# A down projection by seven products over both column halves, in five full K groups and a short last one

## The chip, the cores and the metric

The kernel runs on one core of a Trainium2 chip. The metric is the device time of one execution in microseconds (us). A core has TensorE (PE: matrix products, and PEld, its weight loads), VectorE (DVE), ScalarE (ACT) and GpSimd (POOL), and queues from which transfers are issued; here SyncE's (SP) issues nearly all weight loads and POOL's the transfers that add what they bring to what lies in the destination.

## The reference

Two layers of a decoder trunk over 256 tokens of width 2048, in float32. Layer 0 has a gated DeltaNet beside a latent attention, layer 1 a retention; both end alike, and the change lies in that end alone:

```
u = causal_dwconv(hn @ w_up, conv_w) + conv_b      # w_up: 2048 x 11264, conv width 3
gate, up = jnp.split(u, 2, axis=-1)
h = h + (jax.nn.silu(gate) * up) @ w_down          # w_down: 5632 x 2048
```

A gated per-layer embedding and the next norm follow. With 256 tokens every weight is read about once and used for two blocks of 128 tokens.

## The kernel before

**Precision by splitting.** Each float32 operand is split into a high part (rounded to the matrix engine's format) and a low part (the rest), and a product is the sum of three: high by high, low by high, high by low. For weights `cut` (lines 179 to 195) does it in pieces of 128x1024: ACT casts the piece into a `hi` tile (L188), DVE subtracts it from the raw weights into a `lo` tile (L189). There are four `hi` and four `lo` buffers (`WB`) and four raw buffers of twice that size (`RAWB`).

**The feed-forward layer.** The 5632 inner columns are 44 K tiles of 128. `up` makes them two at a time: each pair takes two `gemm_b` (gate and up half), each of two steps of three yields. One such step is called an *up unit* here: one weight load of 1 MB, two pieces, 16 matmuls of 512 columns (L267) and 16 of 256 (L272). After a `gemm_b` come a copy and an add out of PSUM (L279, L280), a scaling (L282), two scalings on ACT (L1072) and four multiply-adds on DVE (L1074); after both, SiLU, a product (L1084) and the split of the result (L482, L483).

**The down projection** of a group of K tiles runs behind the up projection of the next group. `plain` takes one column block of 512 at a time: for 8 K tiles two units of 24 matmuls (L296, L297, L302), one for each 4 K tiles and both token blocks, and an add into the residual `h` (L1100). `seven` takes two column blocks and 8 K tiles at once as a 2x2 block product (two token blocks, two K halves, two column blocks) by seven block products in place of eight, after Strassen and Winograd. Each is 12 matmuls of 512 columns (L443, L444, L448) and two pieces to split, against one of four left forms made from the activations (`Forms`, L381 to L389) or the activations themselves. The right sides are quadrants of `w_down`, 4 K tiles by 512 columns (1 MB), loaded fresh by SP into a raw buffer (L408), or a running sum T that lies in two tiles: SP writes its first quadrant (L408), and POOL adds further ones by accumulating transfers, two of 512 KB for each quadrant (L412). One product takes B12 + B22, made on DVE (L472).

**The order of the work.** Groups before are K tiles 0-4, 4-12, 12-20, 20-28, 28-36 and 36-44. The four in the middle do column blocks 0 and 1 by `seven` and 2 and 3 by `plain`; the first does all four by `plain`, and the last is a `proj_add` over 8 K tiles that feeds the next norm column by column. `LAG` up units go first; then after each up unit 0.8 units of the group behind it are issued (`SHARE`), in turn one of `plain` and two of `seven`. A scheduler then gives each engine its list in about the order of the code; each engine works its list in order. `then` (before: `following`) starts the next T while the seventh product runs, a whole group ahead of its use.

Of the kernel before, what the change touches and what calls it, by code (L numbers as in the profile page):

```python
# [21 lines left out]
P = 128  # L22
# [10 lines left out]
PSB = 4  # L33
UNIT = 3
LAG = 2
SHARE = 0.8
RATES = [1.7, 1.1, 1.1, 0.95, 2.8]
D = 2048
S = 256
NH = 2  # L40
KB = D // P
CG = 4
EPS = 1e-6
D_FF = 5632
NFT = D_FF // P
# [40 lines left out]
def trunk(ctx: ExitStack, tc: tile.TileContext, a: dict):  # L86
# [12 lines left out]
    V, A, G, T = nc.vector, nc.scalar, nc.gpsimd, nc.tensor  # L99
# [18 lines left out]
    def pb():  # L118
        return psb.tile([P, 512], F32, tag="pb", name=nm("pb"))
# [13 lines left out]
    h = [[None] * CG for _ in range(NH)]  # L133
# [60 lines left out]
    def run(gen):  # L194
        try:
            while True:
                next(gen)
        except StopIteration as e:
            return e.value
# [198 lines left out]
    class Quads:  # L398
# [11 lines left out]
        def plus(self, hh, e):  # L410
            for q in range(2):
                G.dma_start(self.total[q], self.blocks[q, hh, e], accum_op=ALU.add)  # L412

        def begin(self):
            self.put(self.total, 0, 0)
            self.plus(0, 1)

        def fresh(self, hh, e):
            raw = rawp.tile([P, 4, 512], F32, tag="raw", name=nm("raw"))
            dst = [raw[:, 2 * q : 2 * q + 2] for q in range(2)]  # L420
            self.put(dst, hh, e)
            return dst

    def running():
        return [xtile().bitcast(F32).rearrange("p a b c -> p a (b c)") for _ in range(2)]

    def seven(quads, tiles, forms, then):

        c, run_t, fresh, plus = quads.c, quads.total, quads.fresh, quads.plus

        def x(half, i):
            def at(q, k):
                return xl(tiles, 4 * q + 2 * half + k, i)
            return at

        def product(o, left, right, start):
            los = []
            for q in range(2):
                hi, lo = cut(right[q], 2, 512)
                los.append(lo)  # L440
                for k in range(2):
                    l = left(q, k)
                    T.matmul(o, l[0], hi[k], start=start and q + k == 0, stop=False, skip_group_check=True)  # L443
                    last_mm[0] = T.matmul(o, l[1], hi[k], start=False, stop=False, skip_group_check=True)  # L444
                yield
            for q in range(2):
                for k in range(2):
                    last_mm[0] = T.matmul(o, left(q, k)[0], los[q][k], start=False, stop=q + k == 2, skip_group_check=True)  # L448
            yield

        h11, h12, h21, h22 = h[0][c], h[0][c + 1], h[1][c], h[1][c + 1]
        one = pb()
        yield from product(one, forms.left(0), run_t, True)
        V.tensor_sub(h22, h22, one)
        V.tensor_sub(h12, h12, one)
        plus(1, 1)
        acc = pb()
        yield from product(acc, x(0, 0), fresh(0, 0), True)
        V.tensor_add(h11, h11, acc)
        one = pb()  # L460
        yield from product(one, x(1, 0), fresh(1, 0), True)
        V.tensor_add(h11, h11, one)
        yield from product(acc, forms.left(1), run_t, False)
        V.tensor_sub(h12, h12, acc)
        plus(1, 0)
        one = pb()
        b22 = fresh(1, 1)
        yield from product(one, forms.left(3), b22, True)
        V.tensor_sub(h12, h12, one)
        t3 = fresh(0, 1)  # L470
        for q in range(2):
            V.tensor_add(t3[q], t3[q], b22[q])  # L472
        yield from product(acc, forms.left(2), t3, False)
        V.tensor_sub(h22, h22, acc)
        V.tensor_add(h21, h21, acc)
        one = pb()
        yield from product(one, x(1, 1), run_t, True)
        then()
        V.tensor_add(h21, h21, one)

    def put_split(t, k, n, src):
        A.copy(t[:, k : k + n, 0], src)  # L482
# [171 lines left out]
    for g3 in range(3):  # L654
# [14 lines left out]
        ps = run(first_gemm if g3 == 0 else gemm_a(w_in, 0, KB, 4096 + 368 * g3, 368, X))  # L669
# [341 lines left out]
    n = Norm(C_NORM["l0_ffn_norm"])  # L1011
# [44 lines left out]
    def ffn(l, nf, nxt, aside=None):  # L1056
        pin = []
        w_up, w_dn = a[f"l{l}_ffn_w_up"], a[f"l{l}_ffn_w_down"]
        fp = cp.tile([P, N_FFN], F32, name=nm("fp"), tag="fp")
        nc.sync.dma_start(fp, a["par"][:, N_PAR0 + l * N_FFN : N_PAR0 + (l + 1) * N_FFN])  # L1060
        Xf = nf.tiles

        def fc(c):
            return fp[:, c : c + 1]

        def conv(cb, j0):
            ps = yield from gemm_b(w_up, cb, Xf)
            u = joined(ps, nf.bc)
            y = t2((P, 2, S))
            for j in range(2):  # L1070
                ct = j0 + j
                A.activation(y[:, j], u[:, j], AF.Identity, scale=fc(ct + 176), bias=fc(ct + 264))  # L1072
                for lag in range(1, 3):
                    V.scalar_tensor_tensor(y[:, j, lag:], u[:, j, : S - lag], fc(ct + (2 - lag) * 88), y[:, j, lag:], op0=ALU.mult, op1=ALU.add)  # L1074
            return y

        def up(g0, g1, tiles, forms):
            kept = []
            for jp in range(g0, g1, 2):
                tiles.append(xtile())  # L1080
                yg = yield from conv(jp * P, jp)
                yu = yield from conv(D_FF + jp * P, NFT + jp)
                A.activation(yg, yg, AF.Silu)
                V.tensor_mul(yg, yg, yu)  # L1084
                put_split(tiles[-1], 0, 2, yg)
                if forms is not None:
                    kept.append(yg)
                    if len(kept) == 2:
                        forms.add(*kept)
                        kept = []  # L1090

        def down(g0, g1, tiles, forms, quads, then):
            r0, nk = g0 * P, g1 - g0

            def plain(cols):
                for c in cols:
                    ps = [pb() for _ in range(NH)]
                    yield from gemm_a(w_dn, r0, nk, c * 512, 512, tiles, ps)
                    for i in range(NH):
                        V.tensor_add(h[i][c], h[i][c], ps[i])  # L1100

            if forms is None:
                then()
                yield from plain(range(CG))
                return
            fast = seven(quads, tiles, forms, then)
            slow = plain(range(2, CG))
            going = True
            while going:
                going = False  # L1110
                for part in (slow, fast, fast):
                    for _ in range(UNIT):
                        if next(part, part) is not part:
                            going = True
                            yield

        groups = [(max(g - 4, 0), g + 4) for g in range(0, NFT, 8)]
        prev = None
        total = []

        def following(g0):
            if g0 + 8 < NFT:
                if not total:
                    total.extend(running())
                quads.append(Quads(w_dn, g0 * P, 0, total))
                quads[-1].begin()

        quads = []
        for g0, g1 in groups:
            forms = Forms() if 0 < g0 and g1 < NFT else None  # L1130
            cur = (g0, g1, [], forms)
            going = up(g0, g1, cur[2], forms)
            if prev is not None:
                behind_it = down(*prev, quads[-1] if quads else None, partial(following, g0))
                for _ in range(LAG * UNIT):
                    next(going)
                owed = 0.0
                for n, _ in enumerate(going, 1):
                    if n % UNIT:
                        continue  # L1140
                    owed += SHARE
                    if owed >= 1.0:
                        owed -= 1.0
                        for _ in range(UNIT):
                            next(behind_it, None)
                run(behind_it)
            else:
                run(going)
            if g0 == 4 and aside is not None:
                aside()  # L1150
            if g1 + 8 == NFT:
                pin.append(ple_input(l))
            prev = cur
        later(lambda: pin.append(ple_tiles(pin.pop())))
        run(proj_add(w_dn, [(prev[0] * P, prev[2], prev[1] - prev[0])], range(CG), nxt.feed))
        later(nxt.finish)
        return pin[0]
# [337 lines left out]
```

## Time and profile before

| | us |
|---|---|
| median of 3 runs (lowest, highest) | 2880.49 (2878.83, 2880.64) |
| the profiled execution's own time | 2880.58 |
| its span, first to last instruction | 2878.8 |

| engine | busy in the span |
|---|---|
| PE | 2860.8 us, 99% |
| PE weight loads | 2464.2 us, 86% |
| DVE | 2060.9 us, 72% |
| ACT | 1537.8 us, 53% |
| POOL | 121.8 us, 4% |

Busy time is the union of an engine's instructions; neighbours overlap (the next begins before the last one's results are out), so the step from start to start is shorter than an instruction's own time. An average over the program says little on one stage: the feed-forward layers are read by windows.

### The profile page before, as it was taken

What the parts mean: (1) busy time and instruction counts of PE and PEld (TensorE: products, weight loads), DVE (VectorE), ACT (ScalarE), POOL (GpSimd) and SP (SyncE); (2) the same over time, 40 slices, a digit from 0 to 9 for tenths busy, and PEclk for the clock granted to TensorE, in tenths of its full rate; (3) what the DMA queues carried; (4) which work ended last, traced back from release to release, by engine and by line L of the source; (5) the groups of instructions that cost most, each with busy time, mean ns of one, the idle gap of its engine ahead of it and who ended that gap; (6) DMA issues with size and microseconds to landing.
All of it is one profiled execution on the core that took longest, in us unless ns stands there. A gap on an engine that the chain in (4) does not pass through costs nothing.

```text
span 2878.8 us, 38652 instructions
## 1 busy us (share of the span) xinstructions
PE 2860.8 (99%) x15076; PEld 2464.2 (86%) x15076; DVE 2060.9 (72%) x2898; ACT 1537.8 (53%) x2185; POOL 121.8 (4%) x116
## 2 busy tenths in 40 slices
PE   9999999999999999999999999999999999999998
PEld 8899988888888888888888888888888888888887
DVE  7888867778878887656556565655668878788765
ACT  7666655555555555554444444344545555555554
POOL 0111100000000000000000000000000000000000
PEclk9999999999999999999999999999999999999999
DMA  7444445757878787555555555555575777877654
GB/s 236 135 132 131 138 161 194 221 189 203 249 206 235 233 232 225 171 183 192 179 185 186 191 181 182 186 179 189 186 222 185 220 232 223 238 220 223 212 185 145
DMA packets 410040, 562.49 MB, mean 195 GB/s; under 512 B 10752, under 2 KB 266880, under 8 KB 409856
## 3 DMA queue, kind: packets, MB, share of 16 engines
q1 hardware_dynamic: 393376, 530.05, 56.2%
q0 software_dynamic: 13056, 25.17, 5.3%
q10 hardware_dynamic: 3424, 4.79, 0.5%
q8 instruction: 118, 1.93, 0.3%
q14 instruction: 66, 0.54, 0.1%
HBM read 557.87 MB, written 2.10 MB: 195 GB/s over the span
## 4 chain that ended last, share of the span: by engine, by line
PE 98%; DVE 1%; ACT 0%; DMA 0%; issue 0%; POOL 0%; ACTq 0%; POOLq 0%; DVEq 0%
PE pa L267 30%; PE pa L272 16%; PE pa L297 10%; PE pa L296 10%; PE pa L302 10%; PE pb L297 3%; PE pb L296 3%; PE pb L302 3%; PE pb L444 2%; PE pb L443 2%; PE pb L448 2%; PE pb L739 2%; PE pb L316 1%; PE pa L936 1%; PE pb L745 0%; PE pb L1234 0%
## 5 line engine op out<-in xcount | busy, mean ns | idle before, releaser
L189 DVE TENSOR_TENSOR lo<-raw,hi 128x1024 fp32r<-128x1024 f32 (+3 forms) x1140 | 1197.9, 1075 | 555.8 <-ACT hi L188 498.8
L188 ACT CAST hi<-raw 128x1024 fp32r<-128x1024 f32 (+3 forms) x1140 | 1010.0, 931 | 955.5 <-PE pa L297 327.6
L267 PE MATMUL pa<-xg,hi 128*128 128x512 f32 x3840 | 925.9, 392 | 0.0
L267 PEld LDWEIGHTS pa<-xg,hi 128*128 128x128 f32 x3840 | 709.7, 188 | 140.6 <-DVE xg L321 0.3
L296 PE MATMUL pa<-hi,xg 128*128 128x512 f32 (+1 forms) x1348 | 522.8, 388 | 2.0 <-ACT hi L188 1.9
L297 PE MATMUL pa<-hi,xg 128*128 128x512 f32 (+1 forms) x1348 | 521.4, 387 | 0.3 <-DVE xg L321 0.2
L272 PEld LDWEIGHTS pa<-xg,lo 128*128 128x128 f32 x3840 | 490.3, 191 | 16.3
L272 PE MATMUL pa<-xg,lo 128*128 128x256 f32 x3840 | 502.0, 283 | 0.0
L302 PE MATMUL pa<-lo,xg 128*128 128x512 f32 (+1 forms) x1348 | 331.7, 386 | 0.0
L296 PEld LDWEIGHTS pa<-hi,xg 128*128 128x128 f32 x1348 | 253.9, 188 | 50.5 <-ACT hi L188 2.2
L297 PEld LDWEIGHTS pa<-hi,xg 128*128 128x128 f32 x1348 | 253.7, 188 | 49.4 <-DVE xg L321 0.8
L302 PEld LDWEIGHTS pa<-lo,xg 128*128 128x128 f32 x1348 | 250.1, 188 | 47.9
L1074 DVE SCALAR_TENSOR_TENSOR t<-t,fp,t 128x255 f32<-128x255 f32 (+1 forms) x352 | 154.0, 479 | 49.8 <-ACT t L1072 48.5
L297 PE MATMUL pb<-hi,xg 128*128 128x512 f32 x348 | 135.9, 391 | 0.0
L296 PE MATMUL pb<-hi,xg 128*128 128x512 f32 x348 | 135.8, 390 | 0.0
L279 ACT COPY t<-pa 128x512 f32<-128x512 f32 x128 | 75.1, 587 | 76.8 <-PE pa L272 67.6
L412 POOL DMA_DIRECT2D xg<-in_l_ffn_w_down_dram x48 | 57.9, 1206 | 1174.5 <-DVE t L1074 419.9
L1072 ACT ACTIVATE t<-t,fp 128x256 f32<-128x256 f32 x176 | 96.1, 593 | 13.4 <-DVE t L282 13.4
L157 POOL TENSOR_TENSOR small<-small,mhalf 128x1 f32<-128x1 f32 (+2 forms) x38 | 28.8, 757 | 1401.1 <-DVE small L1264 622.6
L280 DVE TENSOR_TENSOR t<-t,pa 128x512 f32<-128x512 f32 x128 | 87.1, 680 | 1.1 <-ACT t L279 1.1
L302 PE MATMUL pb<-lo,xg 128*128 128x512 f32 x348 | 86.5, 389 | 0.0
L321 DVE SCALAR_TENSOR_TENSOR xg<-pb,par,xg 128x256 fp32r<-128x256 f32 x136 | 60.0, 479 | 35.8 <-ACT xg L320 35.0
(280 smaller groups left out, 2233.8 us busy)
## 6 DMA issues: line engine op xcount, KB each, us to landing
raw<-in_l_ffn_w_up_dram SPq DMA_DIRECT2D x176, 1024.0 KB, 5.2
raw<-in_l_w_in_dram SPq DMA_DIRECT2D x128, 1024.0 KB, 5.1
raw<-in_l_ffn_w_down_dram SPq DMA_DIRECT2D x56, 1024.0 KB, 5.2
raw<-in_l_w_out_dram SPq DMA_DIRECT2D x44, 1024.0 KB, 5.1
raw<-in_l_ffn_w_down_dram SPq DMA_DIRECT2D x64, 512.0 KB, 4.9
raw<-in_l_ple_gate_dram SPq DMA_DIRECT2D x32, 1024.0 KB, 5.1
xg<-in_l_ffn_w_down_dram POOLq DMA_DIRECT2D x48, 512.0 KB, 6.8
xg<-in_l_ffn_w_down_dram SPq DMA_DIRECT2D x16, 512.0 KB, 4.6
```

Source lines behind the costliest of these rows:

```text
L188: last_cast[0] = A.copy(vo(hi)[:, c], vi(rk)[:, c])
L189: last_diff[0] = V.tensor_sub(vo(lo)[:, c], vi(rk)[:, c], vo(hi)[:, c].bitcast(F32))
L267: last_mm[0] = T.matmul(ps[:, j], wh, x2, start=first, stop=False)
L272: last_mm[0] = T.matmul(ps[:, j, :S], lo[k][:, j * P : (j + 1) * P], xr(tiles, c * 8 + k)[1], start=False, stop=c == 1 and k == 7)
L279: A.copy(u, ps[:, :, S:])
L280: V.tensor_add(u, u, ps[:, :, :S])
L296: T.matmul(o[i], xh, hi[k], start=begin and k0 + k == 0, stop=False)
L297: last_mm[0] = T.matmul(o[i], xw, hi[k], start=False, stop=False)
L302: last_mm[0] = T.matmul(o[i], xl(tiles, k0 + k, i)[0], lo[k], start=False, stop=end and k0 + k == nkb - 1)
L321: V.scalar_tensor_tensor(t[:, kk, 1], pk, g, t[:, kk, 0].bitcast(F32), op0=ALU.mult, op1=ALU.subtract)
L1072: A.activation(y[:, j], u[:, j], AF.Identity, scale=fc(ct + 176), bias=fc(ct + 264))
L1074: V.scalar_tensor_tensor(y[:, j, lag:], u[:, j, : S - lag], fc(ct + (2 - lag) * 88), y[:, j, lag:], op0=ALU.mult, op1=ALU.add)
```

## The change

Groups become K tiles 0-8, 8-16, 16-24, 24-32, 32-40 (five of 8) and 40-44 (one of 4). Groups 0 to 3 do both pairs of column blocks by `seven`, one after the other; group 4 does blocks 0 and 1 by `seven` and 2 and 3 by `plain`; the last is a `proj_add` over 4 K tiles. So there are nine column halves by seven products in a layer where there were four. The share follows from the group's work: 14 units over the 14 up units left after `LAG`, or 11 over 6 for group 4. One T serves all halves in turn, so a second half's T is begun while the first half's seventh product runs, and used by the next product. T's first product is now the quadrant B11 itself, and each further quadrant (B12, B22, B21) is added after the product that used the sum so far:

| product | right side before | right side now |
|---|---|---|
| 1 | T = B11 + B12 | T = B11 |
| 2 | B11 fresh | B21 fresh |
| 3 | B21 fresh | T, + B12 |
| 4 | T, + B22 | B22 fresh |
| 5 | B22 fresh | T, + B22 |
| 6 | B12 + B22 on DVE | B12 + B22 on DVE |
| 7 | T, + B21 | T, + B21 |

A half reads seven quadrants in place of eight, adds three of them by POOL as before, and makes seven additions out of PSUM in place of nine.

```diff
         def begin(self):
             self.put(self.total, 0, 0)
-            self.plus(0, 1)
...
-    def seven(quads, tiles, forms, then):
-
+    def seven(ready, tiles, forms, then):
+
+        quads = ready.popleft()
...
-        one = pb()
-        yield from product(one, forms.left(0), run_t, True)
-        V.tensor_sub(h22, h22, one)
-        V.tensor_sub(h12, h12, one)
-        plus(1, 1)
         acc = pb()
-        yield from product(acc, x(0, 0), fresh(0, 0), True)
+        yield from product(acc, x(0, 0), run_t, True)
         V.tensor_add(h11, h11, acc)
+        plus(0, 1)
         one = pb()
         yield from product(one, x(1, 0), fresh(1, 0), True)
         V.tensor_add(h11, h11, one)
+        two = pb()
+        yield from product(two, forms.left(0), run_t, True)
+        V.tensor_sub(h22, h22, two)
+        plus(1, 1)
+        b22 = fresh(1, 1)
+        yield from product(two, forms.left(3), b22, False)
+        V.tensor_sub(h12, h12, two)
+        t3 = fresh(0, 1)
+        for q in range(2):
+            V.tensor_add(t3[q], t3[q], b22[q])
         yield from product(acc, forms.left(1), run_t, False)
         V.tensor_sub(h12, h12, acc)
         plus(1, 0)
...
         yield from product(acc, forms.left(2), t3, False)
         V.tensor_sub(h22, h22, acc)
+        yield from product(acc, x(1, 1), run_t, False)
+        then()
         V.tensor_add(h21, h21, acc)
...
-        groups = [(max(g - 4, 0), g + 4) for g in range(0, NFT, 8)]
+        groups = [(g, min(g + 8, NFT)) for g in range(0, NFT, 8)]
+        by_seven = {g0: [0, 2] if n < len(groups) - 2 else [0] for n, (g0, g1) in enumerate(groups[:-1])}
+        jobs = deque((g0, c) for g0, cols in by_seven.items() for c in cols)
...
+        def following():
+            if not total:
+                total.extend(running())
+            if jobs:
+                g0, c = jobs.popleft()
+                ready.append(Quads(w_dn, g0 * P, c, total))
+                ready[-1].begin()
+
+        def down(g0, g1, tiles, forms):
+            fast = chain(*[seven(ready, tiles, forms, following) for _ in by_seven[g0]])
+            rest = [c for c in range(CG) if c - c % 2 not in by_seven[g0]]
+            slow = plain(g0, g1, tiles, rest)
+            parts = [slow, fast, fast] if rest else [fast]
...
-            forms = Forms() if 0 < g0 and g1 < NFT else None
+            forms = Forms() if g1 < NFT else None
...
+                share = sum(7 if c in by_seven[prev[0]] else 2 for c in range(0, CG, 2)) + 2 * (len(by_seven[prev[0]]) == 1)
+                share /= 2 * (g1 - g0) - LAG
```

ACT's list, layer 0, before: from a seventh product's casts of T (the two tiles `xg_5608` and `xg_5609`) on; `raw` pieces are loaded weights, L279 and L1072 belong to the convolution, L388 to the left forms.

```order
L188 CAST hi_7513<-xg_5608 128x1024
L188 CAST hi_7521<-xg_5609 128x1024
L188 CAST hi_7573<-raw_7571 128x1024
L188 CAST hi_7577<-raw_7571 128x1024
L279 COPY t_1341_7533<-pa_7391 128x512
L188 CAST hi_7615<-raw_7613 128x1024
L188 CAST hi_7619<-raw_7613 128x1024
L1072 ACTIVATE t_1342_7537<-t_1341_7533,fp_4995 128x256 x2
L188 CAST hi_7669<-raw_7667 128x1024
L188 CAST hi_7673<-raw_7667 128x1024
L482 CAST xg_7268<-t_1319_7384 128x2x256
L388 CAST t_1345_7554<-t_1343_7548 128x512
```

The next cast of T stands 23 rows after the first of these, behind six further pairs of weight casts.

ACT's list, layer 0, now, at the same step: the casts of T (`xg_5118`, `xg_5119`) for a first half's seventh product, and for the second half's first product.

```order
L187 CAST hi_6450<-xg_5118 128x1024
L187 CAST hi_6458<-xg_5119 128x1024
L1068 ACTIVATE t_1166_6380<-t_1165_6376,fp_4995 128x256 x2
L187 CAST hi_6472<-raw_6470 128x1024
L187 CAST hi_6476<-raw_6470 128x1024
L478 CAST xg_6097<-t_1144_6235 128x2x256
L187 CAST hi_6516<-xg_5118 128x1024
L387 CAST t_1169_6397<-t_1167_6391 128x512
L187 CAST hi_6524<-xg_5119 128x1024
L387 CAST t_1170_6398<-t_1168_6392 128x512
```

Between the two uses of T now stand the casts of one up unit; the second use must wait for the new quadrant, and the left forms' casts (L387) stand behind it.

SP's list, layer 0, before, around the start of a new T:

```order
L169 DMA raw_7571<-in_l_ffn_w_up_dram 128x8x256
L169 DMA raw_7613<-in_l_ffn_w_up_dram 128x8x256
L169 DMA raw_7667<-in_l_ffn_w_up_dram 128x8x256
L169 DMA raw_7709<-in_l_ffn_w_up_dram 128x8x256
L408 DMA xg_5608<-in_l_ffn_w_down_dram 128x2x512
L408 DMA xg_5609<-in_l_ffn_w_down_dram 128x2x512
L169 DMA raw_7753<-in_l_ffn_w_down_dram 128x4x512
L169 DMA raw_7804<-in_l_ffn_w_up_dram 128x8x256
```

SP's list, layer 0, now, around the start of the second half's T:

```order
L168 DMA raw_6470<-in_l_ffn_w_up_dram 128x8x256
L168 DMA raw_6548<-in_l_ffn_w_up_dram 128x8x256
L407 DMA raw_6594<-in_l_ffn_w_down_dram 128x2x512 x2
L168 DMA raw_6617<-in_l_ffn_w_up_dram 128x8x256
L407 DMA xg_5118<-in_l_ffn_w_down_dram 128x2x512
L407 DMA xg_5119<-in_l_ffn_w_down_dram 128x2x512
L168 DMA raw_6698<-in_l_ffn_w_up_dram 128x8x256
L407 DMA raw_6743<-in_l_ffn_w_down_dram 128x2x512 x2
```

The transfer into T moved from between up loads and a plain block to a place with an up load and a fresh quadrant right behind it; ahead of it stand the loads of the next up units and of the second half's first fresh quadrant (`raw_6594`).

## Rows read from the trace of the kernel before

**Rows 1.** The page's head: span; busy time, share and instructions of each engine.
```profile
span 2878.8 us, 38652 instructions
...
PE 2860.8 (99%) x15076; PEld 2464.2 (86%) x15076; DVE 2060.9 (72%) x2898; ACT 1537.8 (53%) x2185; POOL 121.8 (4%) x116
```

**Rows 2.** The page's part 4: the chain that ended last, by engine.
```profile
PE 98%; DVE 1%; ACT 0%; DMA 0%; issue 0%; POOL 0%; ACTq 0%; POOLq 0%; DVEq 0%
```

**Rows 3.** The list of waits, TensorE, whole program: total, times, longest; first of nine.
```profile
PE pa L296 <- ACT hi L188: 1.9, 1, 1.9
```

**Rows 4.** Timeline of TensorE: start, time, then line, operation, tiles, count.
```profile
679.49 0.40 PE L443 MATMUL pb<-hi,xg 128*128 128x512 f32 x1
...
681.33 1.07 PE L448 MATMUL pb<-lo,xg 128*128 128x512 f32 x4
682.24 3.79 PE L267 MATMUL pa<-xg,hi 128*128 128x512 f32 x16
...
687.77 0.40 PE L296 MATMUL pb<-hi,xg 128*128 128x512 f32 x1
...
693.24 3.79 PE L267 MATMUL pa<-xg,hi 128*128 128x512 f32 x16
```

**Rows 5.** Windows, one period of layer 0: busy per engine, PEclk, DMA, GB/s.
```profile
689.87:819.74 129.87, 129.87 (x694) 112.50 (x693) 105.29 (x138) 73.68 (x90) 7.18 (x6) 1.00 0.76 227
```

**Rows 6.** Groups of VectorE in that period: busy, mean ns, idle before.
```profile
L189 DVE TENSOR_TENSOR lo<-raw,hi 128x1024 fp32r<-128x1024 f32 x48 | 57.9, 1219 | 15.2 <-ACT hi L188 15.2
...
L472 DVE TENSOR_TENSOR raw<-raw,raw 128x1024 f32<-128x1024 f32 x2 | 2.4, 1218 | 0.0
```

**Rows 7.** Timeline of VectorE in that period.
```profile
692.53 0.69 DVE L1100 TENSOR_TENSOR t<-t,pb 128x512 f32<-128x512 f32 x1 [2.62 <-PE pb L302]
693.14 2.35 DVE L189 TENSOR_TENSOR lo<-raw,hi 128x1024 fp32r<-128x1024 f32 x2
695.41 0.68 DVE L1100 TENSOR_TENSOR t<-t,pb 128x512 f32<-128x512 f32 x1
```

**Rows 8.** The list of waits of VectorE in that period.
```profile
DVE lo L189 <- ACT hi L188: 15.2, 9, 2.5
DVE t L1100 <- PE pb L302: 5.0, 2, 2.6
DVE t L1074 <- ACT t L1072: 3.4, 3, 1.2
```

**Rows 9.** DMA in that period: queues, then issues with us to landing.
```profile
q1 hardware_dynamic: 21498, 26.24, 60.9%
q0 software_dynamic: 1632, 3.15, 14.9%
...
xg<-in_l_ffn_w_down_dram POOLq DMA_DIRECT2D x6, 512.0 KB, 6.6
xg<-in_l_ffn_w_down_dram SPq DMA_DIRECT2D x2, 512.0 KB, 4.3
```

**Rows 10.** Timeline of VectorE around a seventh product.
```profile
759.43 2.36 DVE L189 TENSOR_TENSOR lo<-xg,hi 128x1024 fp32r<-128x1024 f32 x2
761.70 0.68 DVE L1100 TENSOR_TENSOR t<-t,pb 128x512 f32<-128x512 f32 x1
```

**Rows 11.** Timeline of TensorE at the same place.
```profile
759.53 3.79 PE L267 MATMUL pa<-xg,hi 128*128 128x512 f32 x16
```

**Rows 12.** Line 408 (loads of quadrants), whole program: landing.
```profile
DMA to landing us min/median/max: 3.7/4.9/7.5
```

**Rows 13.** Line 412 (accumulating transfers), whole program: issue ns min/median/max; landing.
```profile
L412 POOL DMA_DIRECT2D xg<-in_l_ffn_w_down_dram x48: 1194/1203/1366, 542.9 to 2666.9; - x48
...
DMA to landing us min/median/max: 5.7/6.8/10.2
```

**Rows 14.** Windows: output projection that feeds the first feed-forward norm.
```profile
462.00:500.00 38.00, 38.00 (x206) 31.68 (x205) 32.61 (x58) 25.96 (x49) 0.70 (x1) 1.00 0.67 219
```

**Rows 15.** Windows: eight microseconds with a high DMA share, layer 0.
```profile
1104.00:1112.00 8.00, 8.00 (x45) 6.92 (x44) 7.72 (x11) 5.00 (x7) 0.00 (x0) 1.00 1.03 263
```

More of the change, by code (lines that the diff above doesn't have):

```diff
@@ L35 @@
 LAG = 2
-SHARE = 0.8
 RATES = [1.7, 1.1, 1.1, 0.95, 2.8]
@@ L465, in seven @@
         plus(1, 0)
[L466 to L472, printed above, removed]
         yield from product(acc, forms.left(2), t3, False)
         V.tensor_sub(h22, h22, acc)
+        yield from product(acc, x(1, 1), run_t, False)
+        then()
         V.tensor_add(h21, h21, acc)
[L476 to L479, printed above, removed]
     def put_split(t, k, n, src):
@@ L1090, in up, with plain @@
                         kept = []
[L1092 to L1107, printed above, removed]
+        def plain(g0, g1, tiles, cols):
+            for c in cols:
+                ps = [pb() for _ in range(NH)]
+                yield from gemm_a(w_dn, g0 * P, g1 - g0, c * 512, 512, tiles, ps)
+                for i in range(NH):
+                    V.tensor_add(h[i][c], h[i][c], ps[i])
+        groups = [(g, min(g + 8, NFT)) for g in range(0, NFT, 8)]
+        by_seven = {g0: [0, 2] if n < len(groups) - 2 else [0] for n, (g0, g1) in enumerate(groups[:-1])}
+        jobs = deque((g0, c) for g0, cols in by_seven.items() for c in cols)
+        ready = deque()
+        total = []
+        def following():
[10 more added lines that the diff above has]
+            parts = [slow, fast, fast] if rest else [fast]
             going = True
@@ L1110, in down @@
                 going = False
-                for part in (slow, fast, fast):
+                for part in parts:
                     for _ in range(UNIT):
@@ L1115, in down @@
                             yield
-        groups = [(max(g - 4, 0), g + 4) for g in range(0, NFT, 8)]
         prev = None
[L1119 to L1129, printed above, removed]
-            forms = Forms() if 0 < g0 and g1 < NFT else None
+        for n, (g0, g1) in enumerate(groups):
+            forms = Forms() if g1 < NFT else None
             cur = (g0, g1, [], forms)
             going = up(g0, g1, cur[2], forms)
[L1133 to L1136, printed above, removed]
+            for _ in range(LAG * UNIT):
+                next(going)
+            if prev is None:
+                following()
+                run(going)
+            else:
+                behind_it = down(*prev)
+                share = sum(7 if c in by_seven[prev[0]] else 2 for c in range(0, CG, 2)) + 2 * (len(by_seven[prev[0]]) == 1)
+                share /= 2 * (g1 - g0) - LAG
                 owed = 0.0
-                for n, _ in enumerate(going, 1):
-                    if n % UNIT:
+                for m, _ in enumerate(going, 1):
+                    if m % UNIT:
                         continue
-                    owed += SHARE
-                    if owed >= 1.0:
+                    owed += share
+                    while owed >= 1.0:
                         owed -= 1.0
@@ L1146, in ffn @@
                 run(behind_it)
-            else:
-                run(going)
-            if g0 == 4 and aside is not None:
+            if n == 1 and aside is not None:
                 aside()
-            if g1 + 8 == NFT:
+            if n == len(groups) - 2:
                 pin.append(ple_input(l))
```

## The prediction

> **What bounds the kernel now.** I read first the page's busy times and its chain. TensorE is busy 2860.8 of 2878.8 us [rows 1] and holds 98% of the chain that ended last [rows 2]. A busy share may hide waits, so the list of waits comes next: TensorE waited nine times for something the profile names, 1.9 us at most [rows 3], and none of these lies in a feed-forward layer. Its granted clock there is 1.00, the 2.4 GHz level [rows 5]. So in the layer that changes the time is a count of matmuls, and two questions are left: how many go, and whether VectorE or the transfers, which get more to do, start to hold TensorE up.
>
> The timeline of TensorE gives the step of each kind of work from start to start [rows 4]: a product of `seven` 679.49 to 682.24, 2.75 us; an up unit 682.24 to 687.77, 5.53; a plain unit 687.77 to 693.24, 5.47. One group's work repeats every 129.87 us (I call it a period); in it VectorE is busy 105.29 us, ScalarE 73.68, and the DMA engines 0.76 of the time at 227 GB/s [rows 5].
>
> **What goes and comes on TensorE.** A column half by `plain` is two blocks of two units: 4 x 5.47 = 21.88. By `seven` it is 7 x 2.75 = 19.25. The difference is 2.63 us. It agrees with the count, 96 matmuls against 84, since 12 matmuls at 5.47/24 = 0.228 are 2.74. A layer has nine halves by seven in place of four, so two layers have ten more: 10 x 2.63 = 26.3 us less. Nothing else on TensorE changes in number. As TensorE sets the end, the whole of it counts unless a new wait gives some back.
>
> **VectorE.** A period in which two halves run by seven has 129.87 - 21.88 + 19.25 = 127.2 us of TensorE. On VectorE the added half has 14 subtractions of 1024 for 8, two sums of 1024 more (L472), and the period has 14 additions out of PSUM for 13. Large ones last 1.22 us [rows 6] but step 2.27/2 = 1.135 back to back, an addition 0.61 [rows 7]. So 8 x 1.135 + 0.6 = 9.7, and VectorE has 115.0 of 127.2 us, 90% where it had 81%. ScalarE gets six casts, about 6 us, 63%. There are four such periods in a layer, eight in all. Of VectorE's idle time now, 15.2 us are waits for a cast [rows 8], and these end with ScalarE, which itself waits until TensorE frees a `hi` buffer: that is slack. 5.0 are for a plain unit's end, which goes, and 3.4 for the convolution on ScalarE, which stays. 115.0 + 3.4 fits. Bursts (two convolution ends and the left forms) are covered by four `lo` buffers, two units of work ahead. Bound below: 0. Bound above: all waits but the 5.0 stay, 15.2 + 3.4 = 18.6 on 115.0, that is 133.6 - 127.2 = 6.4 a period, 51 in all. The waits that the rows show are buffer waits, so I take the lower end, with 1 us for stray ones.
>
> **The turn of T.** This is the one dependency that got much shorter. In layer time let 0 be the end of the sixth product. An up unit ends at 5.5, the seventh product at 8.3, another up unit at 13.8; then the second half's first product needs T again. Its second tile is needed at 13.8 + 0.9 = 14.7 (high part, after half of the 1.84 us of high matmuls [rows 4]) and at 16.1 (low part, 13.8 + 2.3). When is it there? Before, VectorE had split T for a seventh product 2.2 us after the same point (759.53 [rows 11] to 761.70 [rows 10]). Now the sixth product's addition and four multiply-adds of the convolution come ahead or between, 0.6 + 1.6, so 4.5. SP can issue the load of the second tile then. It lands 4.3 us later in this period's median [rows 9], 7.5 in the worst case of line 408 [rows 12]; a cast of about 1.0 and a subtraction of 1.14 follow, and some 1.8 of left forms stand between. So the low part is ready at 4.5 + 4.3 + 3.9 = 12.7, or 15.9 at worst, against 16.1. I take 0. The bounds are 0 and, with the longest landing of any transfer of quadrants, 10.2 [rows 13], 18.6 - 16.1 = 2.5 for each of eight turns, 20 in all. Nothing below 0: no load gets earlier by it. Behind the waiting transfer on SP's queue stand an up load and a fresh quadrant; their uses come two units or more later, and three loads stand ahead of it.
>
> **The other waits added.** An accumulating transfer must now land within two products and two up units where a load alone must at the turn within one of each: 8.3 us more time, against two issues of 1.2 and a landing of 6.6 for 4.3 [rows 9, 13], 4.7 us more work. It has 3.6 us more to spare than the turn, so nothing. POOL has 12 issues a period, 14 us of 127. A sum in PSUM is now carried on after it has been read (products 4 to 7); an up unit of 5.53 stands between read and next write, against an addition of 0.61, so nothing in the eight periods. In group 4 the pace is 11 units to 6 up units, two products can stand side by side, and product 6 must wait until VectorE has read product 5: 0 to 2 us in each layer, I take 1, so 2. The last projection has half as many matmuls between two feeds of the norm; the nearest row is the output projection with only two K blocks to a column and the same feed, where TensorE was busy 38.00 of 38.00 us [rows 14]. It costs 0. Starting with 8 K tiles of up projection alone in place of 4 only moves work.
>
> **DMA.** The plain queue moves 26.24 MB in 60.9% of 130 us, 3.0 us a MB of all engines' time; the accumulating one 3.15 MB in 14.9%, 6.15 a MB [rows 9]. A period now moves 25.2 and 6.3 MB: 76 + 39 = 115 of 127.2 us, a share of 0.90, at 247 GB/s. For 8 us the trace shows 1.03 at 263 GB/s without a wait of TensorE [rows 15]. Loads land in 5 us and are asked for some units ahead, so I take 0. The Trainium skill (Perfetto Trace Analysis, Identifying the Most-Contended Engine) says to judge DMA by bytes moved against what the memory gives, since occupancy of 16 engines misleads. By that rule 247 of the 358 GB/s it gives as a core's share would be 69%, and the transfers would not be a suspect at all. By that rule rival 3 below would have no chance; the rows, where an added byte costs the engines twice a loaded one, leave it one.
>
> **Sum.** The profiled execution took 2880.58 us, its span 2878.8 plus 1.8 around it, 0.1 from the median of 2880.49. 2880.6 - 26.3 + 1 + 0 + 2 + 0 = 2857.3; I say 2857.
>
> **Rivals.** (1) The turn of T comes late: landings stretch to 8 to 10 us as the transfers go from 0.76 to 0.90. From 7.7 us on each us costs 8; at 10.2 it is 20 and the time 2877. Against it: 4.3 in the median at 0.76, and 7.5 as the longest of 80 [rows 9, 12]. (2) The other side: VectorE becomes the bound. Its order holds convolution, split and evacuation in one line, and if its waits stay as long as before (18.6 a period) the work cannot be packed. From 12.2 us of waits a period TensorE stalls; the gain is gone at 15.1; at 18.6 the time is 2854.3 + 51 + 2 = 2907, slower by 0.9%. For it: VectorE has only 12 us of room. Against it: most of those waits are for buffers. (3) The DMA engines hold the pace: if they sustain less than 0.90 a period takes 115/share; at 0.85 it is 135.3, 8.1 more, 65 in all, 2921. For it: three of a half's seven quadrants go the dear way. Against it: 1.03 in [rows 15]. That matmuls saved would turn out to be hidden, or not saved, I give nothing: the count of 120 is fixed by the code and TensorE has no idle time to hide in.
>
> **How the numbers follow.** The forecast, 2854 to 2863, has 64%. Rival 1 has 14%, mostly between 2863 and 2874; rival 2 has 13%, of which 4 in the part that still leaves a gain, 4 about level and 5 slower; rival 3 has 6%, 5 of them slower; 3% are for something unnamed. A measurement of this kernel can tell about 0.2%, 5.8 us, from no change. Faster than 2874.7: 64 + 12 + 4, 80%. Within: 2 + 4 + 1 + 1, 8%. Slower: 12%. The range 2851 to 2876 holds the forecast, nearly all of rival 1 and the mild part of rival 2, some 81%; its lower end is the sum with no loss, 2854.3, less 3 for steps read to 0.02 us.
>
> **What would show it.** In the changed profile: a period of 127 us in place of 129.87 and PE matmuls fewer by 120; VectorE near 115 us in it; DMA share near 0.90. At the turn the first product's casts of T should not end a wait of TensorE; if they do, with T's load behind them, rival 1 holds. Waits of TensorE for `lo` (L188 of the changed kernel) all over the period mean rival 2, waits of ScalarE for raw loads rival 3. The prediction is wrong if TensorE's waits in the two layers sum to more than 20 us.

## The result, and the profile after

The changed kernel took 2853.72 us in the median of four runs (2853.67 to 2855.67). The kernel before, on the same chip, took 2880.46 (2878.83 to 2880.64). The ratio is 0.991, with a 95% interval of 0.9893 to 0.9927. So it is faster by 26.7 us. Executions of one kernel differ by up to 2 us among themselves (before 2878.8 or 2880.4 to 2880.6, changed 2853.7 or 2855.7), so that like with like the gain is some 25 us, and one of the ten executions of the first experiment below, at 10215 us, is left out of its ratio.

The head of the page after, with its chain by engine, answers to [rows 1, 2]. Busy time, share of the span and instructions follow each engine's name.

```profile
span 2852.0 us, 38914 instructions
...
PE 2832.8 (99%) x14956; PEld 2440.3 (86%) x14956; DVE 2163.5 (76%) x3016; ACT 1606.0 (56%) x2253; POOL 194.6 (7%) x176
...
PE 98%; DVE 1%; ACT 1%; DMA 0%; issue 0%; POOL 0%; ACTq 0%; POOLq 0%; DVEq 0%
```

TensorE lost 120 matmuls (15076 to 14956) and 28.0 us of busy time. VectorE gained 102.6 us, ScalarE 68.2 and GpSimd 72.8, and all of that is beside TensorE: the chain is 98% TensorE still.

The list of waits of TensorE over the whole program answers to [rows 3]: total, times, longest.

```profile
PE pa L295 <- ACT hi L187: 1.9, 1, 1.9
...
PE pa L296 <- DVE xg L479: 1.4, 2, 0.7
```

Nine rows again. The second one shown is the only one in the feed-forward layers: 0.7 us in each, at the last projection, where a matmul waits for an activation just evacuated.

Three successive periods of layer 0 answer to [rows 5]; the marks are the starts of VectorE's first addition out of PSUM (L453) in a group's first half, one in a period. Columns: length, then busy time and instructions of TensorE, its weight loads, VectorE, ScalarE and GpSimd, granted clock, DMA share, GB/s.

```profile
590.42:718.06 127.64, 127.64 (x684) 110.64 (x683) 115.53 (x149) 80.17 (x97) 14.45 (x12) 1.00 0.90 248
718.06:845.20 127.14, 127.14 (x682) 110.24 (x681) 114.31 (x147) 80.07 (x96) 14.51 (x12) 1.00 0.89 248
845.20:972.30 127.10, 127.10 (x681) 110.23 (x680) 114.43 (x147) 80.34 (x96) 14.48 (x12) 1.00 0.89 248
```

The period went from 129.87 to 127.1 us with TensorE busy through all of it, at the granted clock of 1.00.

DMA in the second of these periods (each queue's packets, MB and share of the 16 engines' time, then issues with KB each and the median us to landing) answers to [rows 9].

```profile
q1 hardware_dynamic: 20993, 25.17, 59.5%
q0 software_dynamic: 3264, 6.29, 29.2%
...
raw<-in_l_ffn_w_up_dram SPq DMA_DIRECT2D x16, 1024.0 KB, 6.3
...
xg<-in_l_ffn_w_down_dram POOLq DMA_DIRECT2D x12, 512.0 KB, 7.2
xg<-in_l_ffn_w_down_dram SPq DMA_DIRECT2D x4, 512.0 KB, 6.6
```

Twice the accumulating bytes cost nearly twice the time: 6.29 MB in 29.2% of 127.1 us is 5.9 us a MB, against 3.0 for plain loads. The median of 6.6 us for the loads that begin T mixes two kinds. Line 407 at the turn between two halves of one group, in this period, shows

```profile
DMA to landing us min/median/max: 4.6/4.9/5.1
```

At the eight turns these loads land in 3.8 to 5.1 us, as they did before (4.3 [rows 9]). Those that begin T for a next group land in 7.8 to 9.9 us, and T's low part is there some 5 us before it is used.

One wait on VectorE has grown. At product 6 its sum B12 + B22 (L467) waits for the second of the two quadrants (VectorE's list of waits in the second period: total, times, longest):

```profile
DVE raw L467 <- DMA raw<-in_l_ffn_w_down_dram: 3.5, 1, 3.5
```

Before, it waited 4.6 us in the whole program, and not at all in the period of [rows 6]. Now it waits 24.8 us in all, 1.8 to 3.5 in each of the six periods of equal work (three in each layer), and no matmul waits behind it.

### The profile page after: what moved, and what is told of

It is laid out like the page before. It is cut to its first block, busy times and chain, and to the rows that moved or that the text cites. A ratio compares the mean times of both kernels' runs of the same rounds, so it can differ in the third digit from the quotient of the medians.

```text
span 2852.0 us, 38914 instructions
## 1 busy us (share of the span) xinstructions
PE 2832.8 (99%) x14956; PEld 2440.3 (86%) x14956; DVE 2163.5 (76%) x3016; ACT 1606.0 (56%) x2253; POOL 194.6 (7%) x176
## 4 chain that ended last, share of the span: by engine, by line
PE 98%; DVE 1%; ACT 1%; DMA 0%; issue 0%; POOL 0%; ACTq 0%; POOLq 0%; DVEq 0%
PE pa L266 30%; PE pa L271 16%; PE pa L301 10%; PE pa L296 10%; PE pa L295 10%; PE pb L443 4%; PE pb L442 4%; PE pb L447 4%; PE pb L735 2%; PE pb L315 1%; PE pb L296 1%; PE pb L295 1%; PE pb L301 1%; PE pa L932 1%; PE pb L741 0%; PE pb L1232 0%
## 5 line engine op out<-in xcount | busy, mean ns | idle before, releaser
L188 DVE TENSOR_TENSOR lo<-raw,hi 128x1024 fp32r<-128x1024 f32 (+3 forms) x1104 | 1153.7, 1069 | 473.7 <-ACT hi L187 399.9
L187 ACT CAST hi<-raw 128x1024 fp32r<-128x1024 f32 (+3 forms) x1104 | 971.2, 927 | 816.6 <-PE pa L296 328.9
L295 PE MATMUL pa<-hi,xg 128*128 128x512 f32 (+1 forms) x1284 | 497.6, 388 | 2.0 <-ACT hi L187 1.9
L296 PE MATMUL pa<-hi,xg 128*128 128x512 f32 (+1 forms) x1284 | 495.6, 386 | 1.7 <-DVE xg L479 1.4
L301 PE MATMUL pa<-lo,xg 128*128 128x512 f32 (+1 forms) x1284 | 315.8, 386 | 0.0
L295 PEld LDWEIGHTS pa<-hi,xg 128*128 128x128 f32 x1284 | 241.2, 188 | 48.6 <-ACT hi L187 2.2
L296 PEld LDWEIGHTS pa<-hi,xg 128*128 128x128 f32 x1284 | 241.2, 188 | 48.2 <-DVE xg L479 2.3
L301 PEld LDWEIGHTS pa<-lo,xg 128*128 128x128 f32 x1284 | 238.1, 188 | 45.3
L411 POOL DMA_DIRECT2D xg<-in_l_ffn_w_down_dram x108 | 130.7, 1225 | 1187.1 <-DVE lo L188 795.8
L188 DVE TENSOR_TENSOR lo<-xg,hi 128x1024 fp32r<-128x1024 f32 x144 | 173.8, 1218 | 14.5 <-ACT hi L187 14.1
L187 ACT CAST hi<-xg 128x1024 fp32r<-128x1024 f32 x144 | 146.7, 1050 | 58.1 <-PE pb L443 29.9
L443 PE MATMUL pb<-hi,t 128*128 128x512 f32 x288 | 113.1, 393 | 0.0
L442 PE MATMUL pb<-hi,t 128*128 128x512 f32 x288 | 113.0, 392 | 0.0
L279 DVE TENSOR_TENSOR t<-t,pa 128x512 f32<-128x512 f32 x128 | 86.9, 679 | 1.1 <-ACT t L278 1.1
```

What stands on the lines that cost most here:

```text
L187: last_cast[0] = A.copy(vo(hi)[:, c], vi(rk)[:, c])
L188: last_diff[0] = V.tensor_sub(vo(lo)[:, c], vi(rk)[:, c], vo(hi)[:, c].bitcast(F32))
L295: T.matmul(o[i], xh, hi[k], start=begin and k0 + k == 0, stop=False)
L296: last_mm[0] = T.matmul(o[i], xw, hi[k], start=False, stop=False)
L301: last_mm[0] = T.matmul(o[i], xl(tiles, k0 + k, i)[0], lo[k], start=False, stop=end and k0 + k == nkb - 1)
```

## The experiments

**The theories.** A, that of the prediction: time is TensorE's count of matmuls; each half moved from `plain` to `seven` is worth some 2.7 us as long as T is there at the turn, and the new order of the products is what makes it be there. Against it: the order alone, or something beside the count, brought the gain; VectorE was the edge already (rival 2 of the prediction); the DMA engines were (rival 3). The experiments ran in two further sets, in which the kernel before took 2879.17 and 2879.44 us in place of 2880.46, so a difference from the changed kernel's 2853.72 us is uncertain by about 1 us.

**One half in place of two.** The new code, with only the first column half of groups 0 to 3 by seven products: five such halves a layer in place of nine.

```
-        by_seven = {g0: [0, 2] if n < len(groups) - 2 else [0] ...}
+        by_seven = {g0: [0] ...}
```

> The changed kernel, but every full K group does only column blocks 0 and 1 by seven products and blocks 2 and 3 plainly: five halves by seven in a layer in place of nine, eight fewer in both layers. Theory A (the time is the count of matmuls, a half by seven saves 21.88 - 19.25 = 2.63 us): 8 x 2.63 = 21.0 us more than the changed kernel's 2853.7, so 2874.7. Rival (the gain came from the new groups, the short last one above all, and not from the halves): near 2855 to 2860.

Measured: 2875.78 us, ratio to before 0.9989 (0.9979 to 0.9998). The profiled spans are 2873.9 and 2852.0, so eight halves are worth 21.9 us, 2.74 each: the count of 12 matmuls at 0.228 us, to the last digit. Theory A holds, and the second half is where nearly all of the gain lies. TensorE waits nowhere in the layers but for the same 0.7 us at their ends. The new groups bring no gain of their own: this kernel has 24 matmuls fewer than the one before, 5.5 us, and its span is 3.4 us shorter than that of the new order alone (2877.3, third experiment), so the groups cost about 2 us, of which 1.4 are those waits.

**The old order of the products, both halves by seven.** T is again B11 + B12 before the first product that uses it.

```
     def begin(self):
+        self.plus(0, 1)
     ...  (and the old body of seven)
```

> The changed kernel with the old order inside a half: T is B11 + B12 before the first product uses it. At the turn T's load is then followed by an accumulating transfer: 2.4 us of issues and about 7 us to land behind the 4.6 us of the load. In the changed profile the last subtraction of T at a turn ended 14.3 us after the sixth product's end and is needed at 16.1. Theory A (the turn is the tight place, and starting T with one quadrant is what makes it fit): 14.3 + 8.4 to 9.4 is late by 6.6 to 7.6 us at each of eight turns, 53 to 61 us more than 2853.7: 2907 to 2915, and TensorE waits at the turns. Rival (the turn has room enough, or other work fills it): 2853 to 2857.

Measured: 2939.12 us, ratio 1.0206 (1.0186 to 1.0227), 85 us above the changed kernel. The wait at the turn has the predicted size. This is TensorE's longest row of waits (total, times, longest):

```profile
PE pb L443 <- ACT hi L187: 58.1, 16, 5.1
```

58.1 us in eight turns is 7.3 each, two waits to a turn. ScalarE's rows at one turn name what it waits for, the transfers into T:

```profile
646.87 1.04 ACT L187 CAST hi<-xg 128x1024 fp32r<-128x1024 f32 x1 [5.96 <-DMA xg<-in_l_ffn_w_down_dram]
...
652.92 1.04 ACT L187 CAST hi<-xg 128x1024 fp32r<-128x1024 f32 x1 [5.01 <-DMA xg<-in_l_ffn_w_down_dram]
```

But 58 is not 85. The rest is in TensorE's timeline and in the windows of the same stretch (columns as above):

```profile
647.97 0.80 PE L443 MATMUL pb<-hi,t 128*128 128x512 f32 x1 [3.04 <-ACT hi L187]
648.56 0.63 PE L444 MATMUL pb<-hi,t 128*128 128x512 f32 x1
648.99 0.63 PE L443 MATMUL pb<-hi,t 128*128 128x512 f32 x1
...
654.01 0.79 PE L443 MATMUL pb<-hi,t 128*128 128x512 f32 x1 [3.97 <-ACT hi L187]
```

```profile
644.00:650.00 6.00, 2.96 (x12) 1.88 (x10) 1.23 (x1) 1.04 (x1) 0.52 (x1) 0.83 0.98 244
650.00:654.00 4.00, 0.04 (x1) 0.00 (x0) 0.01 (x1) 1.08 (x2) 0.67 (x1) 0.50 0.97 170
654.00:658.00 4.00, 3.98 (x9) 3.14 (x10) 4.00 (x5) 4.00 (x5) 1.20 (x1) 0.50 0.30 44
```

After the waits TensorE's granted clock is 0.50, the 1.2 GHz level, and in 654 to 658 it gets through nine matmuls, 0.43 us apart in place of 0.23. A whole period shows both parts:

```profile
598.30:735.85 137.55, 130.54 (x682) 112.15 (x681) 116.94 (x152) 80.00 (x96) 14.43 (x12) 0.96 0.87 245
```

Against 127.14 it has 7.0 us without work and 3.4 more of work for the same 682 matmuls; 10.4 in each of eight periods would be 83. So the new order (with the eighth quadrant and the two additions that the old one brings back) is worth 85 us here, and the rival that it costs or brings nothing falls. My expectation had the wait and missed the clock.

**The new order alone.** The kernel before (one half by seven in its four middle groups) with T begun as the first quadrant.

```
     def begin(self):
-        self.plus(0, 1)
     ...  (and the new body of seven)
```

> The kernel before with nothing changed but the order inside a half and T's first quadrant (groups and halves as before). Theory A: no matmul less, T begun a whole group ahead: 2880.5, within 1 us. Rival (two additions fewer on VectorE in each half, or shorter PSUM use, give part of the gain): 2 to 5 us less.

Measured: 2880.01 us, ratio 1.0003 (0.9993 to 1.0012). The order brings nothing where only one half of a group runs by seven products, and by the code the plain half beside it gives T's transfers four units more; nothing waited for them before [rows 3]. With the run before it: neither part gains alone, and the two together gain 26.7 us.

**VectorE more loaded.** Behind each product a reduction of 128x512 on VectorE, whose result nobody uses; once in the first kernel, twice in the second.

```
+    spare = cp.tile([P, 1], F32, name="spare", tag="spare")
 ...
+            for _ in range(1):   # 2 in the second
+                V.tensor_reduce(spare, los[1][1].bitcast(F32), axis=AX.X, op=ALU.add)
```

> The changed kernel with one more VectorE instruction behind each product: a sum over 512 columns of its last low part into one spare column that nobody reads, about 0.6 us, 14 in a period, 8.4 us: VectorE has 114.4 + 8.4 = 122.8 of 127.1 us. Theory A (VectorE has room; its waits are for buffers): no more than 3 us above 2853.7. Rival 2 (VectorE cannot be packed that tight): its other waits, 3.4 to 7 us a period, no longer fit, 0 to 3 us a period over and more in bursts: 10 to 40 us more.

> As the run with one more VectorE instruction behind each product, but with two of them: 16.8 us in a period, 114.4 + 16.8 = 131.2 us of VectorE work for 127.1 of TensorE. Theory A (VectorE binds only when its own work is more than TensorE's): 4 us more in each of eight periods and little elsewhere, about 32 us, 2886. Rival 2 (unavoidable waits of 3.4 to 7 us come on top): 60 to 90 us more, 2914 to 2944. If VectorE were far from the bound: no change.

Measured: 2861.76 us (ratio 0.9937, 0.9918 to 0.9957), 8 above the changed kernel; and 2914.13 us (1.0119, 1.0099 to 1.0139), 60 above it. Two periods of the first kernel, then one of the second:

```profile
590.27:718.80 128.53, 128.03 (x684) 110.57 (x683) 123.69 (x163) 79.80 (x97) 14.53 (x12) 1.00 0.88 246
...
2275.87:2402.81 126.94, 126.94 (x681) 110.07 (x680) 122.54 (x161) 79.89 (x96) 14.57 (x12) 1.00 0.89 249
```

```profile
590.65:725.82 135.17, 130.67 (x682) 111.56 (x681) 130.42 (x175) 80.55 (x96) 14.52 (x12) 0.99 0.84 233
```

The period less VectorE's busy time is VectorE's idle time. In the second kernel it is 4.75 us in the period shown and 3.0 to 5.3 in the six periods of equal work, and TensorE idles 4 to 5 us in each of them: there VectorE sets the pace, and 3 to 5 us of its waits are not packed. (The period is 8.0 us longer than the changed kernel's; 4.5 are TensorE's idle time, and its 682 matmuls take 3.5 us longer, at a granted clock of 0.99.) In the first kernel VectorE's idle time is 4.4 to 5.9 us, but TensorE waits only 0 to 1.1 us a period, and not at all in the second row: this kernel stands at the edge. In the second kernel's period VectorE's waits are for ScalarE above all (total, times, longest):

```profile
DVE t L1074 <- ACT t L1072: 2.3, 1, 2.3
DVE lo L188 <- ACT hi L187: 2.0, 1, 2.0
```

In the first kernel's first period they are for a TensorE unit and a load, 2.1 and 1.9, so their cause is not one thing. In the second kernel TensorE waits for VectorE's splits all over the layers (whole program):

```profile
PE pa L271 <- DVE lo L188: 19.9, 21, 2.0
```

Here A's expectation was wrong: it gave VectorE all the idle time of a period, and in the second kernel the rival's reading came out, by which waits are added to the work. In the first the measured 8 lies between the two. The changed kernel is still on A's side: with 3.0 to 5.3 us of such waits, its 114.4 us of work come to 117.4 to 119.7 of 127.1, so some 7 to 10 us of room; the first kernel added 8.1 and stood at the edge.

**More transfers.** Two plain loads of 176 KB behind each product, from ScalarE's queue into spare tiles; a one-column copy of ScalarE orders their reuse. To make room for the tiles, four of eight small buffers (`T1B`) that serve other parts of the layers are given up, which was not measured by itself; so only the feed-forward periods are compared.

```
-T1B = 8
+T1B = 4
 ...
+            for j in range(2):
+                spare.append(spare.popleft())
+                A.copy(spare[-1][:, :1], hi[1][:, :1].bitcast(F32))
+                nc.scalar.dma_start(spare[-1], quads.blocks[0, 0, 0][:, j, :352])
```

> The changed kernel with two more plain loads of 180 KB behind each product, from ScalarE's queue into spare tiles that nobody reads (a one-column copy on ScalarE ahead of each ties it to its place; four small buffers of the mixers are given up for the room, so only the feed-forward periods are compared). 14 x 0.36 = 5.05 MB in a period, at 3.0 us a MB 15.1 us: a DMA share of 0.89 + 0.12 = 1.01 and 288 GB/s. Rival 3 (the engines' busy share is what binds): the transfers hold the pace, periods of 129 to 133 us, 15 to 50 us more in all, waits of TensorE at the turns first. The other reading (bytes against what memory gives, 288 of 358 GB/s): periods stay at 127.1 within 0.5 us.

Measured: 2881.28 us (2874.76 to 2886.28), ratio 1.0001 (0.9991 to 1.0011), 27 above the changed kernel. The profiled execution is the longest of the eight, 2886.28. Its six periods of equal work, then the queues in the first of them:

```profile
592.59:725.30 132.71, 131.14 (x690) 113.13 (x689) 115.80 (x148) 83.59 (x127) 14.45 (x12) 0.99 0.97 277
725.30:856.64 131.34, 128.02 (x681) 110.04 (x680) 114.57 (x147) 82.97 (x124) 14.50 (x12) 1.00 0.98 279
856.64:984.22 127.58, 127.49 (x681) 110.24 (x681) 114.58 (x147) 83.23 (x124) 14.48 (x12) 1.00 1.00 287
2157.37:2294.71 137.34, 131.94 (x689) 113.82 (x688) 115.82 (x149) 83.19 (x127) 14.53 (x12) 0.98 0.93 267
2294.71:2422.84 128.13, 127.37 (x681) 110.18 (x680) 114.49 (x148) 83.33 (x124) 14.50 (x12) 1.00 1.00 286
2422.84:2553.89 131.05, 128.82 (x686) 110.87 (x685) 114.56 (x147) 83.30 (x125) 14.51 (x12) 1.00 0.98 280
```

```profile
q1 hardware_dynamic: 20992, 25.17, 56.9%
q0 software_dynamic: 3311, 6.39, 27.5%
q10 hardware_dynamic: 4032, 5.05, 12.1%
```

5.05 MB at the 3.0 us of [rows 9] are 15.2 us on the 113 that 0.89 of a period stands for: 128 us of engine time, more than the 127.1 there are. In every row the share times the length comes to about 128 us. So full engines explain about 1 us a period; yet the periods are 0.4 to 9.7 us longer than the changed kernel's, and the longest have the lowest shares. What differs between them is one wait. VectorE and TensorE in the longest period:

```profile
2236.84 1.22 DVE L473 TENSOR_TENSOR raw<-raw,raw 128x1024 f32<-128x1024 f32 x1 [8.57 <-DMA raw<-in_l_ffn_w_down_dram]
...
2239.25 0.74 PE L271 MATMUL pa<-xg,lo 128*128 128x256 f32 x4 [4.40 <-DVE lo L188]
```

L473 is the sum B12 + B22 of product 6 (L467 in the changed kernel), which waits for its second quadrant; the split that TensorE needs stands behind it in VectorE's list. The sum's wait in the six periods is 6.9, 5.5, 3.8, 8.6, 4.3 and 5.9 us, and TensorE is without work for 1.6, 3.3, 0.1, 5.4, 0.8 and 2.2; in the two longest periods a lower granted clock (0.99 and 0.98) adds to it. So the transfers do hold TensorE, as rival 3 has it, but through a load that lands late for an engine that works in order, and neither reading of the expectation says how much: at a share of 1.00 and 286 to 287 GB/s TensorE idled 0.1 and 0.8 us, at 0.93 and 267 GB/s 5.4. The Trainium skill (Perfetto Trace Analysis, Identifying the Most-Contended Engine) judges DMA by bytes against the memory's rate rather than by occupancy, and then asks which DMA resource binds. In these rows neither the bytes nor the occupancy of a period tells its length; the wait does. In the changed kernel no wait for transfers reaches TensorE.

**Group 4, the last full one, by seven in both halves too.** It has fewer up units to lay beside its products than the groups before it.

```
-        by_seven = {g0: [0, 2] if n < len(groups) - 2 else [0] ...}
+        by_seven = {g0: [0, 2] for g0, g1 in groups[:-1]}
```

> The changed kernel with both column halves by seven in the fifth full group too: 14 products under the six up units of the short group, 2.3 for each. TensorE has two halves less by plain, 2 x 2.63 = 5.3 us: 2848.4 if nothing waits. Theory A (T's chain needs a split of about 2, two issues of 2.4, a landing of 7 and a cast of 2, 13.4 us, and here two products with their share of up units take only about 10.3): some 3 us late at six uses and 8 at the turn in each layer, about 52 us less the 5.3: near 2900. Rival (the scheduler finds other work, or the waits overlap): 2848 to 2853, which would be faster than both.

Measured: 2892.51 us, ratio 1.0043 (1.0026 to 1.006), 38.8 above the changed kernel, though it has 24 matmuls fewer. TensorE's two longest rows of waits:

```profile
PE pb L442 <- DVE t L469: 15.9, 4, 7.0
PE pa L266 <- ACT hi L187: 10.7, 2, 5.7
```

L469 takes product 5 out of PSUM into `h`, and product 6, which carries the same sum on, must wait for it. In the longest such wait of layer 0 (6.8 us) it stands behind a split of T in VectorE's list; the split waits for ScalarE's cast, and the cast for the accumulating transfer into T:

```profile
1169.97 1.04 ACT L187 CAST hi<-xg 128x1024 fp32r<-128x1024 f32 x1 [5.85 <-DMA xg<-in_l_ffn_w_down_dram]
```

Windows in group 4 of layer 0:

```profile
1110.00:1130.00 20.00, 13.96 (x68) 11.07 (x66) 14.14 (x18) 8.81 (x11) 2.41 (x2) 1.00 0.94 255
1170.00:1190.00 20.00, 15.50 (x57) 11.71 (x58) 12.99 (x18) 10.30 (x12) 0.00 (x0) 0.83 0.55 166
```

Without up units enough between the products TensorE idles 6 and 4.5 us of 20, and the clock falls to a mean of 0.83 in the second. So T's chain was late as theory A has it, and A's condition is cover, not the count alone. None of the seven runs beats the changed kernel.

## Why the prediction came out right, step by step

**TensorE's count, -26.3.** Right and a little small. A half is worth 2.74 us (the first experiment), not 2.63: I took the difference of two steps read from the timeline, and the count of 12 matmuls, which I had beside it, was the better reading. Ten halves are 27.4.

**VectorE, 0 with 1 for stray waits.** 115.0 us forecast, 114.3 to 115.5 measured, and no wait of TensorE for it. The conclusion was right; the margin was not. I had 12.2 us of waits a period as the point from which rival 2 decides, and took all waits to be slack. Where VectorE sets the pace, 3 to 5 us of waits stay, so that the room was some 7 to 10 us: one reduction more per product (122.4 to 123.7 us of VectorE work) already costs 8 us in all.

**The turn of T, 0.** Right, with 1.8 us to spare where I had forecast 3.4 (1.7 to 2.2 at the eight turns). TensorE and VectorE at a turn in the second period (start, time, line, operation, tiles, count):

```profile
758.11 3.79 PE L266 MATMUL pa<-xg,hi 128*128 128x512 f32 x16
...
771.94 0.40 PE L442 MATMUL pb<-hi,xg 128*128 128x512 f32 x1
```

```profile
761.93 1.22 DVE L188 TENSOR_TENSOR lo<-xg,hi 128x1024 fp32r<-128x1024 f32 x1
...
770.10 2.35 DVE L188 TENSOR_TENSOR lo<-xg,hi 128x1024 fp32r<-128x1024 f32 x2
```

The sixth product ends at 758.11, where the first row's up unit starts. VectorE has split T for the seventh product at 763.1, 5.0 later (4.5 forecast). The low part of the new T is there at 772.4, that is 14.3 (12.7 forecast, 15.9 as the worst); needed at 16.1. The second tile's cast on ScalarE waits for its load, as the row shows, and no matmul waits for the cast:

```profile
767.89 1.05 ACT L187 CAST hi<-xg 128x1024 fp32r<-128x1024 f32 x1 [0.62 <-DMA xg<-in_l_ffn_w_down_dram]
```

Rival 1 therefore did not come. At the turns the loads land in 3.8 to 5.1 us, well inside the 7.7 from which I had it cost; of the 1.6 us missing from the forecast margin, 0.6 lie before the second tile's load is issued, 0.3 in its landing and 0.7 behind it.

**The other waits, 2, and strays, 1.** The total was near, the parts were not, and that is luck. Of the 3.6 us between forecast and result (2857.3 and 2853.7), 1.8 are the execution from which I started, 2880.58 where others of the same kernel took 2878.83; its granted clock was low for a moment early in the program, where nothing changed (first row, before; second, changed):

```profile
31.00:35.00 4.00, 4.00 (x15) 3.72 (x15) 3.90 (x13) 2.93 (x10) 0.00 (x0) 0.57 0.37 91
31.00:35.00 4.00, 4.00 (x24) 3.75 (x24) 3.90 (x13) 3.21 (x12) 0.00 (x0) 1.00 0.37 87
```

Another 1.1 are the count above, and 0.7 these waits: 2853.7 less (2878.8 - 27.4) leaves 2.3 where I had 3. Product 6 in group 4 was to wait for VectorE's reading of product 5. TensorE there (layer 0):

```profile
1146.68 1.07 PE L447 MATMUL pb<-lo,t 128*128 128x512 f32 x4
1147.58 1.75 PE L266 MATMUL pa<-xg,hi 128*128 128x512 f32 x7
1149.26 0.50 PE L442 MATMUL pb<-hi,t 128*128 128x512 f32 x1
```

Seven matmuls of the next up unit stand between the two products. I had the units whole; the program order splits them, and 1.7 us cover the addition of 0.61. The last projection, put at 0 by [rows 14], costs the 0.72 us of waits seen above, in each layer, 1.4 in all. No run shows where the other 0.9 lie.

**DMA, 0.** 0.90 at 247 GB/s forecast, 0.89 to 0.90 at 248 measured. Rival 3 is a real mechanism, as the experiment with more transfers shows, but no limit of the share as I had it: a period with 1.00 lost 0.1 us. What I missed is where transfers touch TensorE first, the quadrant that VectorE sums for product 6. I took 0 since loads are asked for some units ahead; this one is late by up to 3.5 us, and in the experiment 3.8 cost TensorE 0.1 us and 4.3 cost 0.8. An estimate from these rows is that some 0.3 us were to spare, the nearest edge of the three.

**What I named as signs:** 120 matmuls fewer, a period of 127, VectorE near 115, a share near 0.90, no wait of TensorE at the casts of T: all came. The sign of a wrong prediction, waits of over 20 us in the two layers, stands at 1.4. The sign that I named for rival 3, waits of ScalarE for raw loads, was not the right one: the wait is VectorE's.

## What to carry to other kernels

Where one engine has no idle time, count its instructions and then ask of every other engine, and of the one dependency that gets shorter, how many us are left; the count gave the gain here, and the margins (7 to 10 us of VectorE, 1.8 us at the turn, less than 1 us at the one load that VectorE waits for) decided that it was kept. An in-order engine's idle time is not all room: take off the waits that its own chain of hops makes. A mean share of the DMA engines does not say which load is late; the list of waits does. And two edits that each bring nothing can belong together: fewer matmuls without the earlier T would have been slower by 2%, and the earlier T without fewer matmuls the same.

## What the runs showed of the hardware that was not expected

- Waits cost TensorE more than their length: 58 us in gaps of 3 to 5 us became 85, because the granted clock was 0.50 after them and nine matmuls took 3.98 us, the time of seventeen at 0.23.
- Accumulating transfers took 5.7 to 6.15 us of all engines' time a MB in the periods shown, against 3.0 for plain ones; over a whole period the DMA engines gave a share of 1.00 at 286 to 287 GB/s, while TensorE idled 0.1 and 0.8 us.
- VectorE was busy 122.54 of 126.94 us, 97%, in a period in which TensorE did not wait at all, and 130.42 of 135.17, 96%, in one in which TensorE waited for it.
